# Memory layer of a two-layer decoder step: the sample's keys and values turned in 32x32 blocks by VectorE in five heads

## The chip, the cores and the metric

The kernel runs on one core of a Trainium2 chip. The metric is the device time of one execution in microseconds (us), the median of several runs. The core has a matrix engine (PE; its weight loads are shown apart as PEld), a vector engine (DVE), a scalar engine (ACT), a general engine (POOL) and a queue from which all transfers of this kernel are issued (SP).

## The reference

One step of a decoder trunk for 256 prompt tokens and 8 x 8 sample tokens, 320 token columns in all: a gated spatial mixer, a gated MLP, an mLSTM memory layer, a second gated MLP, a final norm. The change lies in the memory layer. Cut to it:

```python
p = x @ w_in                                   # q|k, v, o, gates
qk, new_buf = causal_dwconv(qk_pre, conv_buf, conv_w, conv_b)
qk = silu(qk)                                  # 8 heads, DK = 128
sc  = einsum('bhtd,bhsd->bhts', qc, kc) * w_intra
num = w_inter * einsum('bhtd,bhde->bhte', qc, C) + einsum('bhts,bhse->bhte', sc, vc)
h   = num / maximum(abs(den), exp(-m_t))
C_new = decay * C + einsum('bhsd,bhse->bhde', kc * g, vc)
y = (sigmoid(o_pre) * groupnorm(h)) @ w_out
```

`C` is a 128 x 256 matrix for each head and each of the 8 samples; every sample has its own `C`, the prompt starts from zero.

## The kernel before, in words

All activations are held with features on the 128 partitions and tokens along the free axis. Each weight block (128 outputs by up to 1024 inputs) is loaded from HBM into a `raw` buffer (four of them), split by ACT into a rounded high part `wh` (L178) and by DVE into the rest `wl` (L179), three buffers each, and multiplied in three matmuls per input block: `wh` by `xh`, `wh` by `xl`, `wl` by `xh` (L81). In the memory layer the `wl` matmuls come after all the others of a block. Results go to 2 KB PSUM banks: a pool `psm` of three and a pool `psa` of five.

The memory layer (`layer_b`) goes over eight heads. Head `h` takes six weight blocks: q, k, v0, v1, o0, o1, and the work of head `h-1` that follows from its scores (numerators, statistics, state updates, normalised output) is spread between them; in heads 4 to 6 blocks of the output projection follow as well (`early`). PE's order is the order of the program (`pin`). Of the other engines and SP, the order is set at build time by a planner that simulates the program and gives each engine the first instruction in program order that is ready; `issue_after` and `behind` add edges to that order.

What the change touches:

- `qk_epi` (L831 ff): the projection is scaled into a padded row `bpad`, in which each sample has 3 old and 8 new columns (11), convolved into `bcv` (344 columns wide), put through tanh, and packed by two DVE instructions (L849 for the prompt's 256 columns, L851 for the sample's 64) into `qs`. For keys, ACT doubles the sample's 64 columns (L857).
- `v_epi` (L866 ff): two ACT copies bring a v block out of PSUM into `vT`, 320 columns (L868) and the sample's 64 again (L869). The PSUM bank is free after the second.
- `scores` (L879 ff): query-key products, those of the sample in `sc[:, 384:448]`.
- `k_nat` (L946 ff) and `v_nat` (L922 ff), at the end of a head: keys and values are turned by PE, against an identity, so that tokens lie on the partitions. Three transposes of 128 x 128 for the keys (two of the prompt, one of the doubled sample) into one bank `pk` of `psm`, six for the values (three token groups by two feature halves) into two banks `pv` of `psa`. Then ACT and DVE split them into `kgs` (sample, L961 and L962), `kgh`/`kgl` (prompt, L971 and L972), `vh`/`vl` (L932 and L935) and `vb` (L939, L940), and POOL spreads `kgs` into `kgz`. They are used by the next head's numerators and state updates.
- `finish` (L1095 ff): normalised output is turned back by PE (`phn`), gated on DVE in two pieces (L1105, L1106) and split.

Of the kernel before, what the change touches and what calls it, by code (L numbers as in the profile page):

```python
# [17 lines left out]
P = 128  # L18
# [26 lines left out]
def parity(x):  # L45

    return x.rearrange("p (b a) -> p a b", a=2)
# [12 lines left out]
class Net:  # L60
# [627 lines left out]
    def layer_b(self):  # L688
# [5 lines left out]
        with ExitStack() as ctx:  # L694
# [23 lines left out]
                return x.rearrange("p (j e) -> p j e", e=32)[:, :, :16]  # L718


            def gates(rp):

                bif, rst, selr = self.bif, self.rst, self.selr
# [107 lines left out]
            def qk_epi(h, j, ps):  # L831
                s = S[h]
                blk = j * NH + h
                pd = pads[(2 * h + j) % 3]
                ps_ = pd[:, 259:].rearrange("p (b e) -> p b e", e=11)
                nc.gpsimd.tensor_copy(ps_[:, :, 0:3], stt[:, blk, :].rearrange("p (b e) -> p b e", e=3))
                nc.vector.tensor_tensor(pd[:, 3:259], ps[:, :TP], self.rb[:, :TP], op=MULT)
                nc.vector.tensor_tensor(ps_[:, :, 3:11], seg(ps[:, TP:T]), seg(self.rb[:, TP:]), op=MULT)
                nc.gpsimd.tensor_copy(nst[:, blk, 0:24].rearrange("p (b e) -> p b e", e=3), ps_[:, :, 8:11])
                nc.gpsimd.tensor_copy(nst[:, blk, 24:27], pd[:, 256:259])  # L840
                cv = lp.tile([P, NC], F32, tag="cv", name="bcv", bufs=2)
                w = V_CW + blk
# [5 lines left out]
                qs = lp.tile([P, 384], F32, tag="qs", name="qs", bufs=2)  # L848
                q_ = nc.vector.scalar_tensor_tensor(qs[:, :TP], th[:, :TP], 1.0, cv[:, :TP], op0=ADD, op1=MULT)  # L849
                tv, c_ = [x[:, 256:].rearrange("p (b e) -> p b e", e=11)[:, :, 3:11] for x in (th, cv)]  # L850
                s["q_"] = q_, nc.vector.scalar_tensor_tensor(seg(qs[:, TP:T]), tv, 1.0, c_, op0=ADD, op1=MULT)  # L851
                nm = "kh" if j else "qh"
                n = P if j else TP
                hh = lp.tile([P, n], F32R, tag=nm, name=nm, bufs=1)
                ll = lp.tile([P, n], F32R, tag=nm + "l", name=nm + "l", bufs=1)
                if j:
                    nc.scalar.copy(qs[:, T:384], qs[:, TP:T])  # L857
                if j:
# [3 lines left out]
                s["hi"] = self.parts[0]  # L862
                s["qk"[j]] = (qs, hh, ll)
                return self.parts[1]

            def v_epi(h, j, ps):  # L866
                vT = lp.tile([P, 384], F32, tag="vT", name="vTb", bufs=2)
                nc.scalar.copy(vT[:, :T], ps[:, :T])  # L868
                made = nc.scalar.copy(vT[:, T:384], ps[:, TP:T])  # L869
                if h == 1 and not j:  # L870
                    self.behind(S[h]["th"], made)
# [7 lines left out]
            def scores(h):  # L879
# [29 lines left out]
                nc.vector.scalar_tensor_tensor(Qd, seg(q[:, TP:T]), 0.5, seg(pb[:, T:384]), op0=MULT, op1=MULT)  # L909
# [11 lines left out]

            def v_nat(h):  # L922
                s = S[h]
                pv = [self.psa.tile([P, 512], F32, tag="pa", name="pv") for _ in range(2)]
                dsts = [pv[t // 2][:, (t % 2) * DV:] for t in range(3)]
                for t in range(3):
                    for e in range(2):
                        self.tr(dsts[t][:, e * P:(e + 1) * P], s["vT"][e][:, t * P:(t + 1) * P], self.ident)
                for t in range(3):
                    dst = dsts[t]  # L930
                    sc = self.rc[:, t:t + 1]
                    nc.scalar.activation(vh[:, t, :, :P], parity(dst[:, :DV]), AF.Copy, scale=sc)  # L932

                    r, out = (slice(0, P), vl[:, t, :, :P]) if t < 2 else (slice(64, P), vh[64:, t, :, :P])
                    low = nc.vector.scalar_tensor_tensor(out, parity(dst[r, :DV]), sc[r], vh[r, t, :, :P].bitcast(F32), op0=MULT, op1=SUB)  # L935
# [10 lines left out]
            def k_nat(h):  # L946
                s = S[h]
                ks = s["k"][0]
                pool, tag = (self.psm, "pm") if 0 < h < NH - 1 else (self.psa, "pa")
                pk = pool.tile([P, 512], F32, tag=tag, name="pk")  # L950
                for t in range(3):
# [6 lines left out]
                src = pk[:, 2 * P:3 * P]  # L958

                for i, (r, o) in enumerate(((slice(0, 32), slice(32, 64)), (slice(32, 64), slice(0, 32)))):  # L960
                    nc.scalar.activation(kgs[:, i, :], src, AF.Copy, scale=g)  # L961
                    s["ks"] = nc.vector.scalar_tensor_tensor(kgs[o, i, :], src[r], g[r], kgs[r, i, :].bitcast(F32), op0=MULT, op1=SUB)  # L962
                s["kg"] = (kgh, kgl, kgs, kgz)
                if h < NH - 1:
                    k_mask(h)

                def prompt():
                    for t in range(2):
                        g = colsT[:, t, 32 + h:33 + h]
                        src = pk[:, t * P:(t + 1) * P]  # L970
                        nc.scalar.activation(kgh[:, t, :], src, AF.Copy, scale=g)  # L971
                        nc.vector.scalar_tensor_tensor(kgl[:, t, :], src, g, kgh[:, t, :].bitcast(F32), op0=MULT, op1=SUB)  # L972

                if h < NH - 1:
                    prompt()
                return prompt
# [118 lines left out]
            def finish(h):  # L1095
# [3 lines left out]
                for e in range(2):  # L1099
                    pt = self.psa.tile([P, 512], F32, tag="pa", name="phn")  # L1100
                    for t in range(3):
                        self.tr(pt[:, t * P:(t + 1) * P], hn[:, t, e * P:(e + 1) * P], self.ident)
                    y = self.tp.tile([P, T], F32, tag="yf", name="y_b", bufs=2)
                    o = s["o"][e]
                    nc.vector.scalar_tensor_tensor(y[:, :TP], o[:, :TP], 1.0, pt[:, :TP], op0=ADD, op1=MULT)  # L1105
                    nc.vector.scalar_tensor_tensor(pairs(y[:, TP:]), pairs(o[:, TP:]), 1.0, apart(pt[:, TP:384]), op0=ADD, op1=MULT)  # L1106
                    g = gnh[:, 2 * h + e:2 * h + e + 1]
                    yp, h2, l2 = parity(y), halves(yh[:, e, :]), halves(yl[:, e, :])
                    nc.scalar.activation(h2, yp, AF.Copy, scale=g)
# [231 lines left out]
def _lay_out(i):  # L1341
# [29 lines left out]
    a["b_win"] = _blocks(w[:, :48 * P], order)  # L1371
# [65 lines left out]
```

## Time and profile before

| what | value |
| --- | --- |
| time, median of 3 runs | 876.93 us (876.89 to 877.29) |
| the profiled execution: its own time | 876.92 us |
| the profiled execution: span of the trace | 875.2 us |
| instructions | 16934 |
| DVE busy | 671.8 us (77%) |
| ACT busy | 506.0 us (58%) |
| POOL busy | 143.0 us (16%) |
| traffic with HBM | 142.66 MB read, 11.99 MB written |

In the views, a line names the engine, the source line, the operation, the tile written and those read, the shape, and a count; where a mean is given it is in ns. A PE record's duration is that of one matmul from its start to the modelled end; matmuls are pipelined, so the step from one start to the next is shorter than the record.

### The profile page before, as it was taken

What the parts mean: (1) busy time and instruction counts of PE and PEld (TensorE: products, weight loads), DVE (VectorE), ACT (ScalarE), POOL (GpSimd) and SP (SyncE); (2) the same over time, 40 slices, a digit from 0 to 9 for tenths busy, and PEclk for the clock granted to TensorE, in tenths of its full rate; (3) what the DMA queues carried; (4) which work ended last, traced back from release to release, by engine and by line L of the source; (5) the groups of instructions that cost most, each with busy time, mean ns of one, the idle gap of its engine ahead of it and who ended that gap; (6) DMA issues with size and microseconds to landing.
All of it is one profiled execution on the core that took longest, in us unless ns stands there. A gap on an engine that the chain in (4) does not pass through costs nothing.

```text
span 875.2 us, 16934 instructions
## 1 busy us (share of the span) xinstructions
PE 869.1 (99%) x6388; PEld 852.2 (97%) x6388; DVE 671.8 (77%) x1302; ACT 506.0 (58%) x917; POOL 143.0 (16%) x297
## 2 busy tenths in 40 slices
PE   9999999999999999999999999999999999999997
PEld 7899999999999999999999999999999999999997
DVE  7766986588878865559999997878998888786443
ACT  7557554455555543447877776656766555554442
POOL 3530000031000000005433232313003000000000
PEclk9999999999999999999999999999999999999999
DMA  8855645545445555555746777565664554455551
GB/s 264 259 170 167 183 145 180 170 155 171 156 158 169 162 167 157 158 185 150 241 152 225 242 232 219 184 215 170 197 219 145 170 169 149 165 163 166 156 153 60
DMA packets 54949, 155.74 MB, mean 178 GB/s; under 512 B 7460, under 2 KB 12716, under 8 KB 54868
## 3 DMA queue, kind: packets, MB, share of 16 engines
q1 hardware_dynamic: 54868, 154.67, 55.7%
q8 instruction: 50, 0.82, 0.4%
q14 instruction: 31, 0.25, 0.1%
HBM read 142.66 MB, written 11.99 MB: 177 GB/s over the span
## 4 chain that ended last, share of the span: by engine, by line
PE 99%; DMA 0%; DVE 0%; ACT 0%; POOL 0%; issue 0%
PE pm L81 85%; PE pv_a L81 6%; PE num L81 2%; PE pmix L81 1%; PE pcs L81 1%; PE psc L81 1%; PE pCp L81 1%; PE phn L84 1%; PE pv L84 1%; DMA xT<-in_xv 0%; PE pk L84 0%; DVE y_p L677 0%; PE pg L81 0%; PE pc L81 0%; DVE y_s L684 0%; PE pt L84 0%
## 5 line engine op out<-in xcount | busy, mean ns | idle before, releaser
L179 DVE TENSOR_TENSOR wl<-raw,wh 128x1024 fp32r<-128x1024 f32 (+4 forms) x254 | 299.2, 1179 | 112.4 <-ACT wh L178 111.9
L178 ACT CAST wh<-raw 128x1024 fp32r<-128x1024 f32 (+4 forms) x254 | 255.5, 1006 | 217.9 <-PE pm L81 148.9
L81 PE MATMUL pm<-xh,wh 128*128 128x320 f32 x1216 | 356.1, 300 | 0.0
L81 PE MATMUL pm<-xl,wh 128*128 128x320 f32 x1216 | 354.5, 299 | 0.0
L81 PE MATMUL pm<-xh,wl 128*128 128x320 f32 x1216 | 308.8, 299 | 0.0
L81 PEld LDWEIGHTS pm<-xh,wh 128*128 128x128 f32 x1216 | 229.9, 189 | 0.6 <-issue 0.5
L81 PEld LDWEIGHTS pm<-xl,wh 128*128 128x128 f32 x1216 | 229.9, 189 | 0.0
L81 PEld LDWEIGHTS pm<-xh,wl 128*128 128x128 f32 x1216 | 212.0, 189 | 0.0
L81 PE MATMUL pm<-yh_f,wh 128*128 128x320 f32 x352 | 105.2, 299 | 0.0
L81 PE MATMUL pm<-yl_f,wh 128*128 128x320 f32 x352 | 105.2, 299 | 0.0
L81 PE MATMUL pm<-yh_f,wl 128*128 128x320 f32 x352 | 105.2, 299 | 0.0
L81 PEld LDWEIGHTS pm<-yh_f,wh 128*128 128x128 f32 x352 | 66.5, 189 | 0.0
L81 PEld LDWEIGHTS pm<-yl_f,wh 128*128 128x128 f32 x352 | 66.5, 189 | 0.0
L81 PEld LDWEIGHTS pm<-yh_f,wl 128*128 128x128 f32 x352 | 66.5, 189 | 0.0
L581 DVE SCALAR_TENSOR_TENSOR fcv<-fpad,vecs,fcv 128x336 f32<-128x336 f32 x88 | 49.2, 565 | 1.4
L583 ACT ACTIVATE fgl<-fcv 128x256 f32<-128x256 f32 x44 | 18.2, 415 | 37.2 <-DVE fcv L581 37.2
L81 PE MATMUL pm<-yh_a,wh 128*128 128x320 f32 x128 | 38.4, 300 | 0.0
L81 PE MATMUL pm<-yl_a,wh 128*128 128x320 f32 x128 | 38.3, 299 | 0.0
L81 PE MATMUL pm<-yh_a,wl 128*128 128x320 f32 x128 | 38.3, 299 | 0.0
L323 DVE TENSOR_TENSOR xT<-pm,xT 128x320 f32<-128x320 f32 x39 | 19.1, 489 | 24.2 <-PE pm L81 24.2
L81 PE MATMUL pm<-yhb,wh 128*128 128x320 f32 x128 | 35.9, 304 | 0.0
L81 PE MATMUL pm<-ylb,wh 128*128 128x320 f32 x128 | 35.5, 300 | 0.0
(268 smaller groups left out, 1269.2 us busy)
## 6 DMA issues: line engine op xcount, KB each, us to landing
raw<-in_f_up SPq DMA_DIRECT2D x88, 512.0 KB, 3.5
raw<-in_b_win SPq DMA_DIRECT2D x48, 512.0 KB, 3.9
raw<-in_f_dn SPq DMA_DIRECT2D x32, 448.0 KB, 3.4
C<-in_C SPq DMA_DIRECT2D x32, 258.0 KB, 5.4
out_Cs<-C SPq DMA_DIRECT2D x32, 258.0 KB, 4.3
raw<-in_a_win SPq DMA_DIRECT2D x16, 512.0 KB, 3.7
raw<-in_a_wo SPq DMA_DIRECT2D x16, 512.0 KB, 4.2
raw<-in_f_dn SPq DMA_DIRECT2D x16, 512.0 KB, 3.6
```

The lines of the kernel that those rows point to most:

```text
L81: self.pin(self.nc.tensor.matmul(out, lhsT, rhs, start=start, stop=stop, skip_group_check=skip))
L84: self.pin(self.nc.tensor.transpose(out, in_, ident))
L178: self.last_split = self.hold(nc.scalar.copy(wh[:, :kn, :], raw[:, :kn, :]))
L179: self.last_low = nc.vector.tensor_tensor(wl[:, :kn, :], raw[:, :kn, :], wh[:, :kn, :].bitcast(F32), op=SUB)
L323: self.nc.vector.tensor_tensor(x, ps[:, :T], x, op=ADD)
L581: nc.vector.scalar_tensor_tensor(cv, pd[:, i:i + NC], self.vec(w + i * KF), cv, op0=MULT, op1=ADD)
L583: nc.scalar.activation(gl[:, :TP], cv[:, :TP], AF.Gelu_apprx_tanh)
```

## The change

In heads 2 to 6 (`BY_BLOCKS`) PE no longer turns the sample's keys and values. DVE turns them in 32 x 32 blocks (`turn`): the doubled keys from an SBUF tile, each v block straight out of PSUM. When the third is turned, SP writes the three together to a scratch in HBM and reads them back in six transfers that place the blocks as the transposes would have. The sample's parts of `kgs`, `vh` and `vb` are then made from SBUF tiles (`nat`) instead of `pk` and `pv`. So that the reading falls right, the columns of the v weights are reordered on the host, and in all heads `v_nat` writes its transposes in groups of 32 columns.

In all heads `qs` keeps the padded columns (344 wide), which one DVE instruction makes instead of two; consumers take the sample's columns with a stride. The doubled keys get a tile of their own (`ks2`). In `finish` the third transpose is taken against a reordered identity, so that the gating is one DVE instruction over 320 columns. In head 1 ACT's split of head 0's gated output is put behind its part of `v_nat`.

```diff
+BY_BLOCKS = range(2, NH - 1)
...
+            def sample(x):
+                return x[:, TP:].rearrange("p (b e) -> p b e", e=11)[:, :, 3:]
...
-                q_ = nc.vector.scalar_tensor_tensor(qs[:, :TP], th[:, :TP], 1.0, cv[:, :TP], op0=ADD, op1=MULT)
-                s["q_"] = q_, nc.vector.scalar_tensor_tensor(seg(qs[:, TP:T]), tv, 1.0, c_, op0=ADD, op1=MULT)
+                s["q_"] = nc.vector.scalar_tensor_tensor(qs, th, 1.0, cv, op0=ADD, op1=MULT),
...
-                    nc.scalar.copy(qs[:, T:384], qs[:, TP:T])
+                    nc.scalar.copy(s["ks2"].rearrange("p (i b e) -> p i b e", i=2, e=NS), twice(qs))
+                    if by_blocks(h):
+                        turn(h, 0, s["ks2"][:, :64])
...
+                if by_blocks(h):
+                    nc.scalar.copy(vT[:, :TP], ps[:, :TP])
+                    turn(h, 1 + j, ps[:, TP:T])
...
+            def turn(h, i, x):
+                s = S[h]
+                if not i:
+                    s["kv"] = lp.tile([P, 2, 3, 32], F32, tag="kv", name="kv", bufs=1)
+                nc.vector.transpose(s["kv"][:, :, i, :], x)
+                if i == 2:
+                    w = I["turned"][h]
+                    nc.sync.dma_start(w, s["kv"].rearrange("p j i b -> p (j i b)"))
+                    r = w.rearrange("(q a) (j e) -> j a q e", q=4, j=2)
+                    s["nat"] = [lp.tile([P, n], F32, tag="nat" + str(n), name="nat", bufs=1) for n in (P, DV)]
+                    for z in range(0, P, 32):
+                        for n, e in ((0, slice(0, 32)), (1, slice(32, 96)))[:2 - z // 64]:
+                            nc.sync.dma_start(s["nat"][n][z:z + 32].rearrange("p (q e) -> p q e", q=4), r[z // 32 % 2, :, :, e])
...
-                mm(sc[:, 384:448], k[:, TP:384], q[:, TP:T], True, True)
+                mm(sc[:, 384:448], s["ks2"], sample(q), True, True)
...
+                n = 2 if by_blocks(h) else 3
+                for t in range(n):
+                    d = dsts[t][:, :DV].rearrange("p (q e b) -> p e q b", e=2, b=32)
+                    for e in range(2):
+                        self.tr(d[:, e], s["vT"][e][:, t * P:(t + 1) * P], self.ident)
...
+                    dst = parity(dsts[t][:, :DV] if t < n else s["nat"][1])
...
+                if h == 1:
+                    for first in S[0]["yh"]:
+                        self.behind(first, made)
...
-                for t in range(3):
-                    self.tr(pk[:, t * P:(t + 1) * P], ks[:, t * P:(t + 1) * P], self.ident)
+                for t in range(2 if by_blocks(h) else 3):
+                    self.tr(pk[:, t * P:(t + 1) * P], ks[:, t * P:(t + 1) * P] if t < 2 else s["ks2"], self.ident)
...
+                src = s["nat"][0] if by_blocks(h) else pk[:, 2 * P:3 * P]
...
+                        pick = self.ident if t < 2 else self.ident.rearrange("p (j i e) -> p i j e", i=2, e=16)
+                        self.tr(pt[:, t * P:(t + 1) * P], hn[:, t, e * P:(e + 1) * P], pick)
...
-                    nc.vector.scalar_tensor_tensor(y[:, :TP], o[:, :TP], 1.0, pt[:, :TP], op0=ADD, op1=MULT)
-                    nc.vector.scalar_tensor_tensor(pairs(y[:, TP:]), pairs(o[:, TP:]), 1.0, apart(pt[:, TP:384]), op0=ADD, op1=MULT)
+                    nc.vector.scalar_tensor_tensor(y, o, 1.0, pt[:, :T], op0=ADD, op1=MULT)
```

More of the change, by code (lines that the diff above doesn't have):

```diff
@@ L718, in apart, with twice @@
                 return x.rearrange("p (j e) -> p j e", e=32)[:, :, :16]
+            def sample(x):
+                return x[:, TP:].rearrange("p (b e) -> p b e", e=11)[:, :, 3:]
+            def twice(x):
+                return sample(x).unsqueeze(1).to_broadcast([P, 2, NB, NS])
             def gates(rp):
@@ L847, in qk_epi @@
                 s["th"] = nc.scalar.activation(th, cv, AF.Tanh, scale=0.5)
[L848 to L851, printed above, removed]
+                qs = lp.tile([P, NC], F32, tag="qs", name="qs", bufs=2)
+                s["q_"] = nc.vector.scalar_tensor_tensor(qs, th, 1.0, cv, op0=ADD, op1=MULT),
                 nm = "kh" if j else "qh"
@@ L862, in qk_epi @@
                 s["hi"] = self.parts[0]
+                if j:
+                    s["ks2"] = lp.tile([P, P], F32, tag="ks2", name="ks2", bufs=2)
+                    nc.scalar.copy(s["ks2"].rearrange("p (i b e) -> p i b e", i=2, e=NS), twice(qs))
+                    if by_blocks(h):
+                        turn(h, 0, s["ks2"][:, :64])
                 s["qk"[j]] = (qs, hh, ll)
@@ L867, in v_epi, with by_blocks @@
                 vT = lp.tile([P, 384], F32, tag="vT", name="vTb", bufs=2)
[L868 to L871, printed above, removed]
-                S[h].setdefault("vT", []).append(vT)
+                if by_blocks(h):
+                    nc.scalar.copy(vT[:, :TP], ps[:, :TP])
+                    turn(h, 1 + j, ps[:, TP:T])
+                else:
+                    nc.scalar.copy(vT[:, :T], ps[:, :T])
+                    made = nc.scalar.copy(vT[:, T:384], ps[:, TP:T])
+                    if h == 1 and not j:
+                        self.behind(S[h]["th"], made)
+                S[h].setdefault("vT", []).append(vT)
+            def by_blocks(h):
+                return h in BY_BLOCKS
+            def turn(h, i, x):
[11 more added lines that the diff above has]
+                            nc.sync.dma_start(s["nat"][n][z:z + 32].rearrange("p (q e) -> p q e", q=4), r[z // 32 % 2, :, :, e])
             def rows_in(h):
@@ L908, in scores @@
                 Qd = Qz[:, NS:].rearrange("p (b e) -> p b e", e=32)[:, :, :NS]
-                nc.vector.scalar_tensor_tensor(Qd, seg(q[:, TP:T]), 0.5, seg(pb[:, T:384]), op0=MULT, op1=MULT)
+                nc.vector.scalar_tensor_tensor(Qd, sample(q), 0.5, seg(pb[:, T:384]), op0=MULT, op1=MULT)
                 Pf = hp.tile([P, 448], F32, tag="Pf", name="Pf", bufs=1)
@@ L1370, in _lay_out @@
     w = i["b_w_in"][0]
-    a["b_win"] = _blocks(w[:, :48 * P], order)
+    v = w[:, 16 * P:32 * P].reshape(D, NH, 4, 2, 32).transpose(0, 1, 3, 2, 4).reshape(D, 16 * P)
+    a["b_win"] = _blocks(np.concatenate([w[:, :16 * P], v, w[:, 32 * P:48 * P]], axis=1), order)
     g = np.zeros((P, 2 * P), w.dtype)
@@ L1418 @@
     I = {k: nc.dram_tensor("in_" + k, v.shape, F32, kind="ExternalInput").ap() for k, v in arrays.items()}
+    I["turned"] = nc.dram_tensor("turned", (NH, P, 192), F32).ap()
     I["rows"] = nc.dram_tensor("rows", (NH, 392), F32).ap()
```

20 lines of the change are left out of this document (7 added, 13 removed).

## The prediction

> **What bounds the kernel now.** I read the page first: busy times, slices, and the chain that ended last.
>
> ```profile
> PE 869.1 (99%) x6388; PEld 852.2 (97%) x6388; DVE 671.8 (77%) x1302; ACT 506.0 (58%) x917; POOL 143.0 (16%) x297
> ...
> PEclk9999999999999999999999999999999999999999
> ...
> PE 99%; DMA 0%; DVE 0%; ACT 0%; POOL 0%; issue 0%
> ```
>
> PE is busy for 99% of the span at a granted clock in the top tenth of full speed, and the chain back from the last instruction is PE nearly everywhere. The waits of PE, the second view, come to one line, in the first microsecond:
>
> ```profile
> PE pw L81 <- PEq L1417: 0.8, 1, 0.8
> ```
>
> So PE waits for nobody in the memory layer. What leaves PE's queue shortens the span by its whole step, unless something else becomes late; what leaves another engine shortens nothing. The stage itself, by windows (busy us of PE, PEld, DVE, ACT, POOL; clock; DMA share), heads 0 to 4 and then 5 to 7:
>
> ```profile
> 400.00:525.00 125.00, 125.00 (x988) 121.85 (x988) 118.59 (x290) 95.59 (x226) 46.99 (x77) 1.00 0.65 210
> 525.00:640.00 115.00, 115.00 (x908) 111.85 (x907) 95.97 (x232) 76.93 (x166) 23.88 (x33) 1.00 0.62 198
> ```
>
> The first row warns: there DVE works 118.59 of 125 us. It is a close second, and what it gets on top has 6.4 us of room in 125.
>
> **The transposes that go.** In each of five heads PE makes one transpose fewer of the keys (3 to 2) and two fewer of the values (6 to 4): 15 in all. Their price, from a group row and from PE's timeline at the end of heads 3 and 4, which also gives the length of a head, 515.44 - 489.46 = 26 us:
>
> ```profile
> L84 PE MATMUL pv<-ident,vTb 128*128 128x128 f32 x48 | 6.5, 273 | 0.0
> ...
> 489.46 0.49 PE L84 MATMUL pk<-ident,qs 128*128 128x128 f32 x3
> 489.79 0.82 PE L84 MATMUL pv<-ident,vTb 128*128 128x128 f32 x6
> ...
> 515.44 0.49 PE L84 MATMUL pk<-ident,qs 128*128 128x128 f32 x3
> ```
>
> One record lasts 0.273 us, but six end after 0.82, so the step is (0.82 - 0.273) / 5 = 0.109 us; the keys give (0.49 - 0.273) / 2 = 0.109. I take the step: 15 x 0.109 = **1.64 us** off PE.
>
> The Trainium skill, "TensorE: Matmul & The Clock Gate", Part 4, puts a transpose at about 275 ns in a kernel's context, most of it access latency. By that price 15 would give 4.1 us; the trace agrees with the duration, but not with it as a price, since six overlap.
>
> **PE work that is reshaped.** The remaining value transposes write groups of 32 columns, 16 `phn` transposes stream a reordered identity, 8 sample products stream `q` with a stride of 11. No count or width changes. No row shows these patterns; the nearest are the weight matmuls, whose moving operand is read as two interleaved halves:
>
> ```profile
> 490.58 0.30 PE L81 MATMUL pm<-xl,wh 128*128 128x320 f32 x1
> 490.71 0.30 PE L81 MATMUL pm<-xh,wh 128*128 128x320 f32 x1
> ```
>
> One step there is 0.13 to 0.14 us for 320 columns, so interleaved reading costs no more per column than the 0.109 us of 128 plain ones. I take nothing for all three. The other end, as far as I can bound it: 38 value and 16 `phn` transposes each twice as long, 54 x 0.109 = 5.9 us. Below nothing there is no room, since the columns stay the same.
>
> **DVE.** Rows, mean ns:
>
> ```profile
> L849 DVE SCALAR_TENSOR_TENSOR qs<-bth,bcv 128x256 f32<-128x256 f32 x16 | 6.8, 424 | 0.4
> L851 DVE SCALAR_TENSOR_TENSOR qs<-bth,bcv 128x64 f32<-128x64 f32 x16 | 3.4, 215 | 0.0
> L1105 DVE SCALAR_TENSOR_TENSOR y_b<-th_o,phn 128x256 f32<-128x256 f32 x16 | 6.6, 411 | 0.1
> L1106 DVE SCALAR_TENSOR_TENSOR y_b<-th_o,phn 128x64 f32<-128x64 f32 x16 | 3.4, 212 | 0.0
> L291 DVE STREAM_TRANSPOSE trn<-acc 128x320 f32<-128x320 f32 x4 | 2.0, 510 | 0.1
> ```
>
> From 64 to 256 columns costs about 0.20 us, 1.04 to 1.09 ns a column. `qs` in one piece of 344 is then 0.424 + 88 x 0.00109 = 0.52 against 0.64, `y_b` of 320 is 0.411 + 64 x 0.00104 = 0.48 against 0.62: saved 0.12 and 0.14, twice in each head, 0.52 us. Added in five heads: three block transposes of 64 columns. The only such row has 320 columns and 0.510 us; with the same slope 64 columns take 0.510 - 256 x 0.00106 = 0.24; the ends are 0.21 (the 64-column rows) and 0.51. I take 0.24: +0.72 - 0.52 = +0.20 us in a head of 26 us (ends +0.1 and +1.0), and -0.52 in heads 0, 1 and 7. The room of 6.4 in 125 us, 1.3 in 26, covers both ends. The nearest deadline it could miss is that of a weight's low part in head 2:
>
> ```profile
> 441.43 1.23 DVE L179 TENSOR_TENSOR wl<-raw,wh 128x1024 fp32r<-128x1024 f32 x1
> ...
> 443.91 0.84 PE L81 MATMUL pm<-xh,wl 128*128 128x320 f32 x5
> ```
>
> It is done at 442.66, needed at 443.91: 1.25 us of cover, ahead of any block transpose. If the cover goes, PE waits by the excess. The value's turn must also empty its PSUM bank, as ACT did before; it queues behind what DVE has in hand, two `wl` (2.34 us, below) at the worst seen there, and the bank is wanted a block later (503.33 to 506.81, below): 3.5 us.
>
> **ACT.**
>
> ```profile
> L868 ACT COPY vTb<-pm 128x320 f32<-128x320 f32 x16 | 6.7, 417 | 0.8 <-PE pm L81 0.6
> L869 ACT COPY vTb<-pm 128x64 f32<-128x64 f32 x16 | 3.4, 214 | 0.0
> L857 ACT COPY qs<-qs 128x64 f32<-128x64 f32 x8 | 1.9, 240 | 0.0
> ```
>
> In five heads two L869 go (0.43) and two L868 shrink by 64 columns; L857 doubles its columns, some 0.06. A gain of half a microsecond, off the path, worth nothing.
>
> **Transfers.** In five heads, one write of 128 rows of 768 bytes, then four reads of 128 pieces of 128 bytes and two of 128 pieces of 256: 896 packets, 0.23 MB. Their load, from the queue's row; then what the weight splits waited for, and the landings of other transfers of this layer (median us):
>
> ```profile
> q1 hardware_dynamic: 54868, 154.67, 55.7%
> ...
> L178 ACT CAST wh<-raw 128x1024 fp32r<-128x1024 f32 x208 | 216.9, 1043 | 159.9 <-PE pm L81 94.4 <-issue 50.8 <-PE pv_a L81 11.5
> ...
> out_Cp<-Cp SPq DMA_DIRECT2D x8, 129.0 KB, 4.3
> C<-in_C SPq DMA_DIRECT2D x32, 258.0 KB, 5.4
> ...
> L876 SPq DMA_DIRECT2D Mb<-rows x7: 383/424/583, 415.8 to 554.3; - x7
> ...
> DMA to landing us min/median/max: 4.2/4.4/7.2
> ```
>
> One packet takes 0.557 x 16 x 875.2 / 54868 = 0.142 us on average; 896 on 16 engines are at most 8 us by the count, 0.7 by the bytes. A share of 0.65 leaves 9 us idle in 26, and the releasers of the weight splits are PE and issue, no transfer, so loads have time in hand. I take no cost here; if that time goes, a split starts later by the excess. The last two rows are those of `Mb`, seven loads in this layer: 0.424 us to issue, 4.4 to land.
>
> The delicate part is the chain: turn, write, landing, six issues on SP, landing, with SP blocked between (behind it: weight loads, state loads and stores). Head 4, the tightest, by the timelines:
>
> ```profile
> 503.33 0.39 PE L81 MATMUL pcs<-vh,kgz 128*128 128x258 f32 x2
> ...
> 506.29 2.34 DVE L179 TENSOR_TENSOR wl<-raw,wh 128x1024 fp32r<-128x1024 f32 x2
> ...
> 506.81 0.39 PE L81 MATMUL pcs<-vh,kgz 128*128 128x258 f32 x2
> ...
> 516.31 0.35 ACT L961 ACTIVATE kgs<-pk,cols 128x128 fp32r<-128x128 f32 x1
> ...
> 522.14 0.34 DVE L972 SCALAR_TENSOR_TENSOR kgl<-pk,cols,kgh 128x128 fp32r<-128x128 f32 x1
> ...
> 522.95 0.30 PE L81 MATMUL pm<-xh,wh 128*128 128x320 f32 x1
> ```
>
> The second value block ends at about 506.9; DVE is through its `wl` at 508.6, the turn ends near 508.9. A write like `out_Cp` lands 4.3 later, 513.2; the last of six issues of 0.42 starts at 515.3; like `Mb` it lands 4.4 later: **519.7**. The first `kgs` runs on ACT at 516.31 now, 3.4 us before. If it keeps its place, ACT stands, and behind it stand `kgh`, then DVE's second `kgl`, now done at 522.48, which frees the PSUM bank that head 5's first block takes at 522.95: 0.47 us of cover. What speaks against that: in these heads `kgh`, `kgl` and the prompt's `vh` no longer share an input with `kgs`, so the planner, which issues what is ready, can put them ahead; and then nothing on PE's side waits for the blocks until the next head's numerators, two weight blocks on. The edits cost nothing in that case, which I take as likelier, because only a planner that thinks the blocks landed by 516 keeps the old place.
>
> The Trainium skill, "DMA: Bandwidth & Descriptors", Anatomy of one DMA, has a fixed cost of about 2.0 us. Two such landings would bring the blocks at about 515 and free ACT at once; the rows of this stage, 4.3 and 4.4, speak against it.
>
> **The sum.** The profiled execution took 876.92 us (span 875.2, 1.7 around it), the median is 876.93. 876.92 - 1.64 = **875.3 us**, by its unknowns of a few tenths 874.9 to 875.7.
>
> **Rivals.**
> 1. *The blocks come late* and ACT's queue stands, as above. With the landings of 4.3 and 4.4, head 4 alone stalls: 3.4 - 0.47 = 2.9 us, 875.3 + 2.9 = 878.2. With 5.4, the median of `C`, for both, the lateness is 5.5 in head 4. In heads 5 and 6 an output block gives 3.3 us more between value and `kgs`:
>
> ```profile
> 539.31 0.39 PE L81 MATMUL pcs<-vh,kgz 128*128 128x258 f32 x2
> ...
> 552.07 0.35 ACT L961 ACTIVATE kgs<-pk,cols 128x128 fp32r<-128x128 f32 x1
> ...
> 557.89 0.34 DVE L972 SCALAR_TENSOR_TENSOR kgl<-pk,cols,kgh 128x128 fp32r<-128x128 f32 x1
> ...
> 558.71 0.30 PE L81 MATMUL pm<-xh,wh 128*128 128x320 f32 x1
> ```
>
> 12.76 against 9.50, so 2.2 late there, less the same cover (558.71 - 558.23 = 0.48): 5.0 + 1.75 + 1.75 = 8.5 us, 883.8. Heads 2 and 3 use that bank two blocks later and stay covered. From 1.64 us of stall on the kernel is slower than before, from 3.4 by over 0.2%.
> 2. *DVE becomes the bound* of heads 2 to 4: what PE loses it waits for. For it, 118.59 of 125; against it, PE's empty list of waits and +0.20 us a head. It gives 876.9.
> 3. *Reshaped reading or writing* on PE costs a few ns to 0.109 us a transpose: 875.4 to 881.2, by its likelier low part 876.
> 4. *Each transpose gives its whole record*, 15 x 0.273 = 4.1: 872.8. The overlap of six records speaks against it. That is the skill's price as above.
>
> **Chances.** A measurement of this kernel tells about 0.2%, 1.75 us, from no change: below 875.2 is faster, above 878.7 slower. Forecast 0.55, of which a third falls below 875.2 by the unknown tenths; rival 1 with a total stall up to 3.4 us 0.12, above it 0.17; rival 2 0.05; rival 3 0.07, of which 0.03 above 878.7; rival 4 0.04. Faster 0.23, same 0.57, slower 0.20. From 874.8 to 880.0, which cuts off rival 4, the long part of rival 1 and the far end of rival 3, the range holds 0.8.
>
> **What would show it.** Right: PE's list of waits stays at its first line, `pv` counts 38 and `pk` 19, the span falls by 1.6. Rival 1: ACT idle before `kgs` or `vh` with a DMA as releaser, PE idle at the first block of the next head. Rival 2: PE idle before `pm` of a `wl` half, released by DVE. Rival 3: `pv` or `phn` steps over 0.109 us. The forecast is wrong if PE shows idle time of more than a few tenths anywhere in heads 2 to 7.

## The result, and the profile after

| | before | after |
| --- | --- | --- |
| time, median | 876.93 us | 882.09 us (881.54 to 883.61, 6 runs) |
| ratio to before, 95% interval | | 1.0061 (1.0048 to 1.0074) |
| span of the profiled execution | 875.2 us | 881.7 us |

The changed kernel is slower by 0.6%, 5.2 us; the forecast was 875.3 and its range ended at 880.0. From the page of the changed kernel, busy times and the chain that ended last:

```profile
PE 870.2 (99%) x6373; PEld 851.3 (97%) x6373; DVE 675.5 (77%) x1285; ACT 504.4 (57%) x907; POOL 147.0 (17%) x297
...
PE 90%; DVE 5%; DMA 3%; issue 1%; SPq 1%; ACT 1%; POOL 0%; ACTq 0%; DVEq 0%
```

PE has 15 matmul records fewer, as forecast, but the chain, PE alone before, now runs through DVE and transfers for a tenth. PE's waits, one line before, are ten (what waited <- what it waited for: us in total, times, longest; line numbers are each kernel's own, L82 here is before's L81):

```profile
PE pm L82 <- DVE kgl L1010: 1.6, 1, 1.6
PE num L82 <- DVE vl L970: 1.1, 2, 0.6
PE pw L82 <- PEq L1456: 0.8, 1, 0.8
PE num L82 <- DVE vh L970: 0.6, 1, 0.6
PE pcs L82 <- ACT Cp L1102: 0.5, 1, 0.5
PE psc L82 <- DVE C L1119: 0.4, 1, 0.4
PE pm L82 <- DVE C L1119: 0.4, 1, 0.4
PE pm L82 <- ACT yhb L1147: 0.3, 1, 0.3
PE pm L82 <- DVE ylb L1148: 0.2, 1, 0.2
PE pm L82 <- DVE o_b L1127: 0.2, 1, 0.2
```

The bank of rival 1 leads the list, but most of it is something else. What released `kgl` is in the chain between 470 and 530 us (start, length, what; SPq is an issue in SP's queue):

```profile
483.56 0.16 DVE kv L896
...
484.01 5.76 DMA turned<-kv
489.79 0.32 SPq L904
...
492.61 1.68 DMA nat<-turned
...
494.44 0.41 ACT kgs L999
...
511.99 0.16 DVE kv L896
...
522.32 0.41 ACT kgs L999
...
526.66 0.35 DVE kgl L1010
```

Read from the top: head 3's last turn ends at 483.72, the write lands at 489.8, six reads are issued by 492.6 and land at 494.3: 10.6 us. In head 4 the turn ends at 512.15 and `kgs` runs at 522.32. Each time ACT's `kgs` starts at once, so ACT stood at it. The views of waits say the same of ACT and of SP's queue:

```profile
ACT kgs L999 <- DMA nat<-turned: 5.1, 3, 2.4
ACT vh L967 <- DMA nat<-turned: 3.1, 2, 1.8
```

```profile
SPq L904 <- DMA turned<-kv: 16.5, 5, 4.8
```

**Where the time came from.** For every kernel below I took from PE's timeline the start of each head's first weight block, and its shift against before (464.38, 490.36, 522.95, 558.71, 594.47 and, for the first whole output block after head 7, 634.59 us), less the shift that the kernel has at head 2 already (-0.24 to +0.61; there PE's order is the same in all). Microseconds:

| kernel | head 3 | head 4 | head 5 | head 6 | head 7 | output |
| --- | --- | --- | --- | --- | --- | --- |
| changed kernel | -0.32 | -0.41 | +4.10 | +3.88 | +4.19 | +6.32 |
| no_blocks | 0.00 | 0.00 | 0.00 | 0.00 | 0.00 | +2.15 |
| blocks_34 | +0.01 | -0.32 | +2.01 | +2.11 | +2.11 | +4.24 |
| blocks_56 | 0.00 | 0.00 | 0.00 | -0.33 | +0.38 | +2.52 |
| no_reads | +2.15 | +3.52 | +3.74 | +3.41 | +3.09 | +5.53 |
| tail_order | 0.00 | 0.00 | 0.00 | 0.00 | 0.00 | +0.06 |
| late_use | -0.33 | +0.85 | +1.75 | +1.42 | +1.10 | +3.23 |
| late_tail | -0.32 | +0.14 | +1.03 | +0.70 | +0.38 | +0.44 |
| turns_only | +0.02 | +0.02 | +0.02 | +0.02 | +0.02 | +0.08 |
| transfers_only | 0.00 | +0.36 | +0.35 | +0.35 | +0.36 | +0.42 |
| keys_late | 0.00 | +0.65 | +1.26 | +1.26 | +1.26 | +1.33 |
| late_tail_256 | -0.33 | +0.54 | +0.53 | +0.21 | -0.12 | -0.05 |
| load_first | -0.32 | +0.59 | +1.50 | +1.17 | +0.84 | +0.90 |
| keys_first | -0.31 | +1.14 | +2.33 | +2.01 | +1.68 | +1.74 |
| late_tail_56 | +0.02 | +0.02 | +0.01 | -0.32 | -0.64 | -0.57 |

A column is the shift at the start of that head, so what a head costs is the step to the next column. In the changed kernel head 2 gives 0.32, head 4 costs 4.5, head 6 0.3, and head 7, where no block is turned, 2.1. The ends of the kernels, after PE's last work, differ by up to 0.8 us for no reason that I found; the medians hold that too.

### The profile page after: what moved, and what is told of

It reads as the page before. It is cut to its first block, busy times and chain, and to the rows that moved or that the text cites. A ratio compares the mean times of both kernels' runs of the same rounds, so it can differ in the third digit from the quotient of the medians.

```text
span 881.7 us, 16933 instructions
## 1 busy us (share of the span) xinstructions
PE 870.2 (99%) x6373; PEld 851.3 (97%) x6373; DVE 675.5 (77%) x1285; ACT 504.4 (57%) x907; POOL 147.0 (17%) x297
## 4 chain that ended last, share of the span: by engine, by line
PE 90%; DVE 5%; DMA 3%; issue 1%; SPq 1%; ACT 1%; POOL 0%; ACTq 0%; DVEq 0%
PE pm L82 78%; PE pv_a L82 6%; DMA turned<-kv 2%; PE num L82 2%; DVE wl L180 1%; PE pmix L82 1%; DMA nat<-turned 1%; SPq L904 1%; DVE C L1119 1%; PE pCp L82 1%; PE pcs L82 0%; PE pw L82 0%; DVE ylb L1148 0%; PE psc L82 0%; DVE bcv L854 0%
## 5 line engine op out<-in xcount | busy, mean ns | idle before, releaser
L180 DVE TENSOR_TENSOR wl<-raw,wh 128x1024 fp32r<-128x1024 f32 (+4 forms) x254 | 302.7, 1193 | 111.4 <-ACT wh L179 110.5
L82 PE MATMUL pm<-xh,wh 128*128 128x320 f32 x1216 | 356.3, 300 | 1.6 <-DVE kgl L1010 1.6
L82 PE MATMUL pm<-xl,wh 128*128 128x320 f32 x1216 | 354.5, 299 | 0.0
L82 PE MATMUL pm<-xh,wl 128*128 128x320 f32 x1216 | 308.8, 299 | 0.0
L82 PEld LDWEIGHTS pm<-xh,wh 128*128 128x128 f32 x1216 | 229.9, 189 | 2.6 <-DVE kgl L1010 1.8
L82 PEld LDWEIGHTS pm<-xl,wh 128*128 128x128 f32 x1216 | 229.9, 189 | 0.1
L82 PEld LDWEIGHTS pm<-xh,wl 128*128 128x128 f32 x1216 | 212.0, 189 | 0.0
L82 PE MATMUL pm<-yh_f,wh 128*128 128x320 f32 x352 | 105.2, 299 | 0.0
L82 PE MATMUL pm<-yl_f,wh 128*128 128x320 f32 x352 | 105.2, 299 | 0.0
L82 PE MATMUL pm<-yh_f,wl 128*128 128x320 f32 x352 | 105.2, 299 | 0.0
L82 PEld LDWEIGHTS pm<-yh_f,wh 128*128 128x128 f32 x352 | 66.5, 189 | 0.0
L82 PEld LDWEIGHTS pm<-yl_f,wh 128*128 128x128 f32 x352 | 66.5, 189 | 0.0
L82 PEld LDWEIGHTS pm<-yh_f,wl 128*128 128x128 f32 x352 | 66.5, 189 | 0.0
L82 PE MATMUL pm<-yh_a,wh 128*128 128x320 f32 x128 | 38.4, 300 | 0.0
L82 PE MATMUL pm<-yl_a,wh 128*128 128x320 f32 x128 | 38.3, 299 | 0.0
L82 PE MATMUL pm<-yh_a,wl 128*128 128x320 f32 x128 | 38.3, 299 | 0.0
L82 PE MATMUL pm<-yhb,wh 128*128 128x320 f32 x128 | 36.2, 305 | 0.9 <-DVE C L1119 0.4
L82 PE MATMUL pm<-ylb,wh 128*128 128x320 f32 x128 | 35.6, 301 | 0.2 <-DVE ylb L1148 0.2
```

The source lines that it names most:

```text
L82: self.pin(self.nc.tensor.matmul(out, lhsT, rhs, start=start, stop=stop, skip_group_check=skip))
L180: self.last_low = nc.vector.tensor_tensor(wl[:, :kn, :], raw[:, :kn, :], wh[:, :kn, :].bitcast(F32), op=SUB)
```

## The experiments

**Which heads: no_blocks, blocks_34, blocks_56.** One line each, with (), (3, 4) or (5, 6); the rest of the change (wide `qs` and `y_b`, grouped transposes, reordered identity) stays.

```diff
-BY_BLOCKS = range(2, NH - 1)
+BY_BLOCKS = ()
```

> BY_BLOCKS is empty: all transposes stay on PE, the padded queries and keys, the merged gating and the reordered identity stay changed. Theory A (the turned blocks arrive late in heads 3 and 4 and stop ACT) expects the 4.5 us lost between the starts of head 4 and head 5 to be gone, and with it the gain of 0.33 us a head; what is lost in head 7 (1.2 us ahead of the numerators, 0.9 after them) should stay, since DVE's order in head 7 comes from the other edits: 876.9 + 2.1 = 879.0. Theory B (the merged and padded edits give the planner a worse order everywhere) expects the loss in heads 3 and 4 to stay: 881 or more. Theory C (strided reading and writing on PE) expects pv or phn steps above 0.109 us.

> Blocks in heads 3 and 4 alone. Theory A: both late arrivals stay, 876.9 - 0.66 + 4.5 + 2.1 = 882.8. Theory B: as with no blocks, less 0.66.

> Blocks in heads 5 and 6 alone, where an output block gives the transfers 3.3 us more. Theory A: no ACT wait for a transfer above 1 us, 876.9 - 0.66 + 2.1 = 878.3. Theory B: 881.

Measured: 879.68 us, ratio 1.0030 (1.0019 to 1.0041); 881.74, 1.0050 (1.0035 to 1.0065); 879.45, 1.0025 (1.0015 to 1.0034). Without a single block the kernel still loses 2.15 us, all in head 7, and nothing in heads 2 to 6: so the reshaped PE patterns cost nothing, and there is a second cause that the blocks have no part in. The blocks of 3 and 4 cost 2.1 by head 7, those of 5 and 6 0.4. Both runs missed their sums, by 1.1 us. In blocks_34 head 4 loses 2.3 us and not the 4.5 of the changed kernel; up to there the two differ only in the blocks of head 2, which therefore add to the loss; and in blocks_56 ACT waits for the blocks all the same, up to 3.1 us at `vh`, and head 6 loses 0.7.

**Head 7: tail_order.** VectorE in head 7 of the kernel before, of the changed kernel, then of tail_order (start, length):

```profile
617.74 0.48 DVE L935 SCALAR_TENSOR_TENSOR vl<-pv,rc,vh 128x256 fp32r<-128x256 f32 x1
...
619.15 1.23 DVE L179 TENSOR_TENSOR wl<-raw,wh 128x1024 fp32r<-128x1024 f32 x1
```

```profile
621.90 1.23 DVE L180 TENSOR_TENSOR wl<-raw,wh 128x1024 fp32r<-128x1024 f32 x1
623.16 0.34 DVE L1000 SCALAR_TENSOR_TENSOR kgs<-pk,cols,kgs 32x128 fp32r<-32x128 f32 x1
623.54 0.48 DVE L970 SCALAR_TENSOR_TENSOR vl<-pv,rc,vh 128x256 fp32r<-128x256 f32 x1
624.05 0.49 DVE L970 SCALAR_TENSOR_TENSOR vh<-pv,rc,vh 64x256 fp32r<-64x256 f32 x1
```

```profile
617.57 0.48 DVE L970 SCALAR_TENSOR_TENSOR vl<-pv,rc,vh 128x256 fp32r<-128x256 f32 x1
618.09 0.49 DVE L970 SCALAR_TENSOR_TENSOR vh<-pv,rc,vh 64x256 fp32r<-64x256 f32 x1
...
618.99 1.23 DVE L180 TENSOR_TENSOR wl<-raw,wh 128x1024 fp32r<-128x1024 f32 x1
```

In the changed kernel a `wl` of 1.23 us that nobody needs yet stands ahead of `vl` and `vh`, which the numerators need (`num <- vl`, `num <- vh` above); in the other two it stands behind `vl`. A second `wl` stands ahead of the second `y_b`, from which `yhb` and `ylb` are made. That this order costs the time is what tail_order tests. Why the planner chose it is my reading, which no run tests: the merged instructions are 0.12 and 0.14 us shorter, DVE is free that much before its next input is ready, and the planner, which gives an engine the first instruction that is ready, fills the hole with `wl`. tail_order is no_blocks with two edges.

```diff
             self.prefetch(0, self.used + 2)
+            self.behind(self.last_low, S[h]["ks"])
...
                         rest = self.take()[0]
+                        self.behind(self.last_low, gated)
```

> No blocks, as the run no_blocks, and two edges on DVE in head 7: the weight split that the planner put between the two key splits goes behind the second, and the one that it put ahead of the second gating goes behind it. If the 2.4 us of no_blocks come from these two long splits placed into a gap that the merged instructions left, PE waits for nobody in head 7 again: 877.2. If the merged and padded edits cost by themselves, 879.7 stays.

Measured: 877.79 us, ratio 1.0009 (1.0000 to 1.0019). The 2.15 us are gone (+0.06 left), and PE's list is again the one line in the first microsecond.

**Late blocks: no_reads, late_use.** no_reads leaves the six reads out; `nat` is a constant.

```diff
-                    s["nat"] = [lp.tile([P, n], F32, tag="nat" + str(n), name="nat", bufs=1) for n in (P, DV)]
-                    for z in range(0, P, 32):
...
+                    s["nat"] = nats
```

> Blocks in heads 2 to 6; DVE turns them and SP writes them, but the six transfers that read them back are left out, and the sample's keys and values are a constant. Theory A: nothing to wait for, the whole gain shows beside the loss in head 7: 876.9 - 1.64 + 2.1 = 877.4. If it is DVE's added work or the planner's order instead (theory B), heads 3 and 4 still lose 4 us: 881.

Measured: 882.56, 1.0061 (1.0046 to 1.0076), a miss. It doesn't test what it was made for: with `nat` always there, the planner takes `kgs`, the sample's `vh` and a `wl` ahead of `o_b`, which frees a bank. DVE, then PE (a bracket at the end of a row is the wait before it and what ended it):

```profile
464.60 1.95 DVE L180 TENSOR_TENSOR wl<-raw,wh 128x1024 fp32r<-128x1024 f32 x1
```

```profile
467.01 0.40 PE L82 MATMUL pm<-xh,wh 128*128 128x320 f32 x1 [2.12 <-DVE o_b L1124]
...
467.68 0.47 PE L82 MATMUL pm<-xl,wh 128*128 128x320 f32 x1
467.94 0.47 PE L82 MATMUL pm<-xh,wh 128*128 128x320 f32 x1
```

So the place in the queue decides, even when no block is late. Of the 3.5 us lost by head 4 the wait is 2.1; the rest lies in PE's slow steps behind it (last section). late_use leaves the data alone and changes the order only: ACT and DVE take the prompt's `kgh`, `kgl`, `vh`, `vl` first, then the sample's `vh` and, in `sample_part`, `kgs` and `kgz`.

```diff
+                    if t == 2 and by_blocks(h):
+                        for x, y, z in zip((made, low), after, s["last"]):
+                            self.behind(x, y)
+                            self.behind(x, z)
...
+                if by_blocks(h):
+                    s["sample_part"](after)
```

> The changed kernel, with ACT and DVE forced to take the prompt's keys and values of a head first and what is read from the blocks after them, so that a late block holds up neither the PSUM bank of the keys nor the prompt's values. Late blocks as the cause: heads 3 and 4 lose little, what stays is head 7's 2.1 to 2.4 less 1.64 us: 877.5 to 878. If something else costs in heads 3 and 4: 881 or more.

> Both: blocks used late, and the two edges in head 7. If the two causes are all there is, the forecast of the step is met: 877.0 - 1.64 = 875.4, and PE's list of waits holds its first line alone. If a third is hidden, 877 or more.

Measured: late_use 880.34, 1.0036 (1.0023 to 1.0049), between what late blocks alone (877.5 to 878) and something else (881) had been given; late_tail, which has tail_order's edges too, 878.12, 1.0012 (1.0002 to 1.0021). ACT no longer waits for `nat`, and 6.32 - 3.23 = 3.1 us are back. That is what the changed order wins on balance: the wait in ACT's queue goes, and what the new order costs by itself (keys_late, below) is already taken off. But late_tail should have gained 1.64 by head 7 and stands at +0.38: 2.0 us more are lost, in heads 3 and 4.

**Another queue for the write: pool_write.**

```diff
-                    nc.sync.dma_start(w, s["kv"].rearrange("p j i b -> p (j i b)"))
+                    nc.gpsimd.dma_start(w, s["kv"].rearrange("p j i b -> p (j i b)"))
```

> The changed kernel, with the write to the scratch issued from POOL's queue; the reads stay on SP. If the write lands late because it stands in SP's queue behind two weight loads and state loads of 1 MB, it lands here in 2 to 3 us instead of 5 to 5.8 in heads 3 and 4, ACT's waits for the blocks shrink from 8 us to under 4, and the kernel takes 879 to 880. If the lateness lies in the transfer itself, nothing changes: 882.

Measured: 895.33, 1.0211 (1.0195 to 1.0226), a miss: the write lands no sooner (median 5.8 us against 5.0 in the changed kernel), and ACT waits longer for the blocks. The run doesn't isolate the queue: POOL itself stood 13.3 us before the five writes, and PE's steps are slow behind three of its waits (last section).

```profile
ACT vh L967 <- DMA nat<-turned: 15.5, 5, 4.0
```

**The third cause: turns_only, keys_late, late_tail_256.** turns_only puts DVE's turns alone back into tail_order; keys_late puts late_use's order of the keys alone into it, with the sample's turned keys copied out of their bank (the second diff).

```diff
+                        nc.vector.transpose(s["kv"][:, 0, :], s["ks2"][:, :64])
...
+                        nc.vector.transpose(S[h]["kv"][:, 1 + j, :], ps[:, TP:T])
```

```diff
+                    src = lp.tile([P, P], F32, tag="nat", name="nat", bufs=1)
+                    nc.scalar.copy(src, pk[:, 2 * P:3 * P])
```

> tail_order with only VectorE's share of the change put back: three block transposes of 64 columns in each of heads 2 to 6, into a tile that nobody reads; no write, no reads, keys and values still turned by PE. Theory D (VectorE's own load is the third cause, 3 x 0.24 us a head in a stretch where it is busy 25.3 of 25.6 us): PE waits of 0.3 to 0.4 us on DVE's C and o_b in heads 3 and 4, some 2 us together, as in late_tail; head 5 begins 2 us later than in tail_order, time 879.8. Theory K (the third cause is the keys' sample part coming late, so that POOL's kgz falls beside a wl and stretches it): no such waits, head 5 begins within 0.3 us of tail_order, time 877.8. A value between says that each has a share.

> tail_order with only the order of late_use: in heads 2 to 6 ACT copies PE's turned sample keys out of the bank and kgs, and with it POOL's kgz, comes behind the prompt's parts; no block transposes, no transfers. Theory K: POOL's kgz meets wl, wl of 1.5 to 1.9 us where it took 1.21, PE waits on C and o_b in heads 3 and 4, head 5 begins about 2 us later than in tail_order, time 879 to 880. Theory D: no waits on C and o_b, head 5 begins within 0.3 us of tail_order, time 877.8. ACT has a copy of 0.3 us more a head, which neither theory gives a price.

> late_tail with the blocks in heads 2, 5 and 6 alone: heads 3 and 4 are turned by PE as before, so that neither the late blocks nor the third cause can act there. Three heads gain 0.33 us each. If the third cause belongs to heads 3 and 4, with no output block between, no PE wait is left in heads 2 to 7 and it takes 877.8 - 1.0 = 876.8, within 0.2% of before. Rival: VectorE's lag from head 2 reaches head 3, or heads 5 and 6 have a stall of their own that late_tail hid behind an earlier one: 877.5 to 878.5, with PE waits on C or o_b there.

Measured: 877.14, 1.0002 (0.9993 to 1.0011); 878.36, 1.0014 (1.0005 to 1.0023); 877.05, 1.0000 (0.9991 to 1.0008). turns_only loses nothing anywhere: **DVE's own load is not the cause by itself**, the room that the prediction counted was there. keys_late loses 1.26 in heads 3 and 4, less than the 2 expected, and PE waits for `ks`, not for `C` or `o_b`. DVE and POOL there, then DVE of turns_only:

```profile
497.07 1.48 DVE L181 TENSOR_TENSOR wl<-raw,wh 128x1024 fp32r<-128x1024 f32 x1
498.48 1.35 DVE L855 SCALAR_TENSOR_TENSOR bcv<-bpad,vecs,bcv 128x344 f32<-128x344 f32 x1
```

```profile
496.34 3.11 POOL L1045 TENSOR_TENSOR kgz<-kgs,mk 128x512 fp32r<-128x512 f32 x2 [14.24 <-DVE kgs L1015]
```

```profile
496.20 1.22 DVE L181 TENSOR_TENSOR wl<-raw,wh 128x1024 fp32r<-128x1024 f32 x1
497.33 0.61 DVE L855 SCALAR_TENSOR_TENSOR bcv<-bpad,vecs,bcv 128x344 f32<-128x344 f32 x1
```

`kgz` on POOL, moved to a later time, runs beside `wl` and `bcv`, and all of them get longer: together 1.0 us on DVE, after which the keys' `ks` is late for the scores. PE's wait, then DVE of keys_late a head earlier:

```profile
PE psc L83 <- ACT ks L871: 0.8, 2, 0.4
```

```profile
479.45 1.22 DVE L181 TENSOR_TENSOR wl<-raw,wh 128x1024 fp32r<-128x1024 f32 x1
480.59 0.51 DVE L859 SCALAR_TENSOR_TENSOR qs<-bth,bcv 128x344 f32<-128x344 f32 x1
```

These rows show a rival that no run tests: the planner put a `wl` of 1.2 us ahead of the keys' `qs`, from which `ks` is made, in both heads; in turns_only `qs` runs at 478.40 and the `wl` follow it. Each of the two delays, 1.0 and 1.1 us, is longer than what a head loses, 0.65 and 0.61. So keys_late shows that the order of the keys costs 1.26 us, and not that the meeting of `kgz` and DVE alone does.

late_tail_256 gains as expected in heads 5 and 6, but head 3 loses 0.87 behind the blocks of head 2. It shows another share, in ACT's timeline and SP's; behind it SP of turns_only:

```profile
470.95 1.04 ACT L179 CAST wh<-raw 128x1024 fp32r<-128x1024 f32 x1 [2.55 <-DMA raw<-in_b_win]
```

```profile
461.08 2.71 SPq L904 DMA_DIRECT2D nat<-turned  x6
...
465.29 0.43 SPq L158 DMA_DIRECT2D raw<-in_b_win  x1
```

```profile
459.73 0.39 SPq L159 DMA_DIRECT2D raw<-in_b_win  x1
```

SP stands until the write has landed, and the weight load behind the reads goes out some 5.5 us late; ACT then waits 2.55 for it.

**Transfers alone, and the queue mended: transfers_only, load_first, keys_first.** transfers_only is turns_only with the write and the reads, of which nothing is used. load_first is late_tail with the reads behind that weight load (the diff). keys_first also writes the keys' block by itself and early, so that `kgs` keeps its old place.

```diff
-                            nc.sync.dma_start(s["nat"][n][z:z + 32].rearrange("p (q e) -> p q e", q=4), r[z // 32 % 2, :, :, e])
+                                self.behind(nc.sync.dma_start(s["nat"][n][z:z + 32].rearrange("p (q e) -> p q e", q=4), r[z // 32 % 2, :, :, e]), load)
...
                     o_made = o_epi(h, 1, blk())
+                    if by_blocks(h):
+                        S[h]["read"](self.last_load)
```

> turns_only with the write and the six reads put back, of which nobody uses the result; keys and values are still turned by PE and used in the old order, so no late use and no late kgz. Theory S: SP stands behind the write's landing, the weight load behind the reads is issued about 5 us later, ACT waits for raw at about 470, C and o_b are late, PE waits in heads 3 and 4 add up to 1 to 2 us, time 878 to 879 against 877.1. Theory K: the transfers alone cost nothing on PE's path, head 5 begins within 0.3 us of turns_only, time 877.1.

> late_tail with one edge on SP's queue: the six reads are issued behind the weight load of the next head's o0 block (in late_tail that load stands in the queue behind the reads, which wait for the write to land; it goes out at 465.6 where turns_only has 459.7, and ACT waits 1.9 us for it at 470.9). Theory S (the third cause is that SP's queue stands and the weight load behind it is late): no ACT wait on raw, VectorE's C and o_b in time, the waits of psc and pm in heads 3 and 4 gone, head 5 begins 2 us earlier against its own head 3 than in late_tail, time 878.1 - 2.0 = 876.1; with the 0.7 us by which the ends of these kernels differ 875.5. Theory K (POOL's late kgz stretches wl and the instructions beside it, as in keys_late): the ACT wait goes, but some 1.2 us of PE waits stay, time 877.3. Both ends below or near before; only the first would be a gain.

> All five heads, with both roads to VectorE's lag closed at once: the keys' block is written by itself as soon as it is turned and read behind the values' write (so the reads wait less and kgs is not late), the values' two reads go behind the weight load of load_first, kgs comes right behind yhb and ylb as before the change, ACT and VectorE take the prompt's vh ahead of the sample's, wl of the next head behind vl in heads 3 and 4, and the two edges of tail_order in head 7. If the third cause is made of these two, SP's queue and kgz beside wl, no PE wait over 0.1 us is left in heads 2 to 7, head 7 begins 1.64 us earlier than in turns_only and it takes 877.14 - 1.64 = 875.5 (with the 0.7 us by which the ends of these kernels differ, up to 876.2). Rival: the blocks of the keys land later than 465.1, 491.2 and 517.2, ACT stands before kgs as in the changed kernel, and it takes 877 to 879.

Measured: 877.79, 1.0009 (1.0000 to 1.0018); 878.01, 1.0012 (1.0003 to 1.0021); 878.52, 1.0015 (1.0006 to 1.0024). The transfers alone cost 0.36 us, in head 3, where the same load is late:

```profile
471.05 1.04 ACT L180 CAST wh<-raw 128x1024 fp32r<-128x1024 f32 x1 [1.25 <-DMA raw<-in_b_win]
```

load_first missed its gain (+0.84 at head 7 against late_tail's +0.38): ACT's wait shrinks to two of 0.3, but in head 2 the reads go out 1.3 us later than in late_tail_256, `kgz` with them, and in both heads it falls on DVE's work. DVE of load_first, where `wl` and `bcv` have the lengths of keys_late:

```profile
497.89 1.48 DVE L180 TENSOR_TENSOR wl<-raw,wh 128x1024 fp32r<-128x1024 f32 x1
499.30 1.35 DVE L854 SCALAR_TENSOR_TENSOR bcv<-bpad,vecs,bcv 128x344 f32<-128x344 f32 x1
```

keys_first missed too, the other way: in heads 2 and 3 `kgz` is in time and DVE undisturbed, but with eight issues around two landings SP's weight loads are late in three heads, and `vh` and `wl` behind them:

```profile
ACT wh L179 <- DMA raw<-in_b_win: 6.5, 3, 2.8
```

As I read it, late loads and late `kgz` are two ways to the same delay of DVE, and in heads 2 to 4 I closed one only by opening the other. The two runs that take them alone, transfers_only and keys_late, lose 0.36 + 1.26 = 1.6, near late_tail's 2.0. That doesn't prove the split: keys_late's loss has a second possible cause, the `wl` ahead of `qs`, which late_tail doesn't have. How the 2.0 divides stays open.

**The change where there is room: late_tail_56.** late_tail with `BY_BLOCKS = (5, 6)`.

> late_tail with the blocks in heads 5 and 6 alone, where an output block stands between the values and kgs: in late_tail_256 these two heads gained 0.32 and 0.33 us with no stall, while head 2 gave 0.33 and cost head 3 0.87. Theory (the stalls belong to heads 2 to 4, where SP's queue and VectorE have no room): no PE wait left in heads 2 to 7, head 7 begins 0.65 us earlier than in turns_only against the same start, time 877.1 - 0.65 = 876.5, with the 0.7 us by which ends differ 876.4 to 877.1; that is the only version so far that could beat both kernels, by less than 0.2%. Rival: head 5's own late weight load stalls head 6 once nothing earlier hides it: 877.2 or more, with a wait of psc or pm on DVE there.

Measured: 876.68 us (876.25 to 877.33), before 877.13 on the same chip, ratio 0.9995 (0.9985 to 1.0004). The two heads give 0.33 and 0.32, three steps of 0.109 each, PE's list is again the one line of before, and the sum is within the measurement.

## Why the prediction was wrong, by its steps

- **The transposes that go** (15 x 0.109 us): right. A head without a stall gives 0.32 to 0.33 in the changed kernel, blocks_56 and late_tail_56. That 15 give 4.1 (rival 4) is refuted.
- **Reshaped PE work**, taken as nothing: right; no_blocks has all of it and is at 0.00 up to head 7 (rival 3 falls).
- **DVE's sizes**: right. From the changed kernel's groups (count, busy us, mean ns):

```profile
L858 DVE SCALAR_TENSOR_TENSOR qs<-bth,bcv 128x344 f32<-128x344 f32 x16 | 8.2, 515 | 0.3
L1144 DVE SCALAR_TENSOR_TENSOR y_b<-th_o,phn 128x320 f32<-128x320 f32 x16 | 7.1, 476 | 0.0
L896 DVE STREAM_TRANSPOSE kv<-pm 128x64 f32<-128x64 f32 x10 | 2.4, 244 | 0.0
```

  0.52, 0.48 and 0.24 had been worked out, and turns_only shows that the room covers them (rival 2, as priced from load, falls). What failed is that the saving in head 7 was put down as work off the path: with the shorter instructions the planner took a `wl` first, and that order cost 2.15 us (no_blocks has it, tail_order takes it away). The prediction had no step for that.
- **The chain of the blocks**: the sum was right, its parts not. From the turn to the blocks 4.3 + 2.1 + 4.4 = 10.8 had been taken, and 10.6 came, as 5.8 for the write, 2.8 of issues and 1.7 for the last read. The turn ahead of it was sized too short: 2.0 us after the value block had been taken, and it ended 3.1 us after it in head 3 (480.67 to 483.72) and 4.7 in head 4 (507.47 to 512.15), behind `C` and two `wl`. The Trainium skill, "DMA: Bandwidth & Descriptors", Anatomy of one DMA, has about 2.0 us fixed for a transfer issued by GpSimd. The reads, issued from SP, come near it (median 1.9); the write, 96 KB, doesn't, from SP (median 5.0) or, in pool_write, from POOL (5.8).
- **The step that failed** is the next: "The edits cost nothing in that case, which I take as likelier, because only a planner that thinks the blocks landed by 516 keeps the old place." The planner thought so: it put `kgs` where it had been but for one `kgh` and `vh`, and SP's reads early. Rival 1 was the case: taking it out gives 3.1 us back (late_use), and in blocks_34 head 4 lost 2.3, where the rival had worked out 2.9 for that head alone. The measured 882.09 lies near the rival's long end, 883.8, by luck: 2.1 of it come from head 7, which is no part of the rival.
- **What is late next** was wrong too. For heads 2 and 3 the prediction looked only at the bank that `kgl` frees, and called them covered. The stalls that follow head 3's late blocks are at the numerators' `vl` (0.6 us), `Cp` (0.5) and `C` (0.4), before any bank.
- **SP's queue**, "loads have time in hand", left out the load's place in the queue: SP stood 16.5 us, and a weight load was issued at 465.32, as late as in late_tail_256. In the changed kernel itself no wait of ACT for that load is on the list; what it costs is known from transfers_only alone, 0.36 us.

The changed kernel's 6.32 us at the output, then: -1.64 for the transposes, +2.1 for head 7, and +5.8 in heads 3 to 6 for the blocks and what follows from them. late_use gives 3.1 of these 5.8 back. The 2.7 left (its +1.10 at head 7 and the 1.64 it should have gained) are not shown to be the same loss in the changed kernel: late_use loses 1.2 us in head 3, where the changed kernel gains 0.1, and its own order delays `kgz`. What the changed kernel's trace does show of `kgz` is two `wl` of 1.95 us beside it in head 4, at 496.91 and 524.78, the second ahead of the `kgl` that PE waits for. The forecast had the first term alone.

## What to carry to other kernels

Work taken off a bound engine counts only if what replaces it lands before the place where its consumers already stand in their queues; list every queue on the way, the issuing one too, and for each what stands behind the waiting instruction. Where a planner sets the order, a shorter instruction can change the order: read the order that it makes before a saving is put down as free. And test "this engine is too full" by adding its work alone, as turns_only did, before believing it.

## What was not expected of the hardware

- **DVE and POOL.** `wl`, 1.21 us alone, took up to 1.95 beside POOL's `kgz` (1.95 in no_reads, 1.48 in keys_late), `bcv` 1.35 against 0.6, and the two `kgz` 2.4 to 3.1 against 2.1. Instructions with one input from PSUM were not stretched. POOL and DVE before the change, where `kgz` runs beside them:

```profile
492.66 2.04 POOL L985 TENSOR_TENSOR kgz<-kgs,mk 128x512 fp32r<-128x512 f32 x2 [11.87 <-DVE kgs L962]
```

```profile
493.07 0.34 DVE L962 SCALAR_TENSOR_TENSOR kgs<-pk,cols,kgs 32x128 fp32r<-32x128 f32 x1
...
493.97 0.48 DVE L935 SCALAR_TENSOR_TENSOR vl<-pv,rc,vh 128x256 fp32r<-128x256 f32 x1
```

  The Trainium skill, "SBUF — State Buffer", Who interferes with whom, has it that a VectorE instruction with two SBUF inputs contends with a GpSimd instruction that reads SBUF. The rows agree, and moving `kgz` by 3 us was enough to meet it.
- **PE after a pause.** In no_reads PE's steps after a wait of 2.12 us are 0.26 to 0.27 us where they are 0.136 otherwise, as the rows at 467.68 and 467.94 show; the granted clock falls with them, to 0.51 between 467.3 and 470.8 us, from 1.00 before. In pool_write the same follows waits of 2.88, 2.42 and 1.47 us (granted clock 0.63 to 0.67 in the 3 to 3.5 us behind them), but not one of 1.36; in the changed kernel, after one of 1.56 us, the steps stayed at 0.14. So no single length of wait decides it here, and a stall of 1.5 to 3 us can cost more than itself.
